# A bidirectional state-space scan: its within-chunk decay tables made during the attention and parked in DRAM

## The chip, the cores and the metric

The kernel runs on one core of one Trainium2 chip. The metric is the device time of one execution in microseconds (us), as the median of several runs; the profile is one more execution, recorded instruction by instruction. The engines are called PE (matrix products), DVE (vector work), ACT (activation functions and copies), POOL (the general engine, which also issues some DMAs) and SP (which issues most DMAs).

## The reference, cut to what matters

The program is two layers of a hybrid encoder: 1040 tokens (16 of them learned meta tokens), width 1024, all in float32. One input projection feeds four groups of 512 channels each: pooling, a 2-D Fourier transform, a bidirectional state-space scan (SSD) and attention. The group outputs are gated and go through one output projection, and the residual is added. The scan in one direction is

```
da  = dt * a                       # per token and head, 8 heads of 64 channels
cs  = cumsum(da)                   # within a chunk
L   = exp(cs[t] - cs[s])  for s <= t, else 0
y_diag = ((C B^T) * L) @ (x * dt)  # within the chunk
y_off  = C h_prev * exp(cs[t])     # from the chunks before
h      = h_prev * exp(cs[end]) + B^T (x * dt * exp(cs[end] - cs))
```

It runs forwards and backwards with separate dt and a, and the two are summed. For one chunk and one head the within-chunk part of both directions is one table of token s by token t, "decay times step size", multiplied by the product of B and C. That table depends on dt and a alone, not on x, B or C.

## The kernel before, in words

Chunks have 104 tokens (QC), ten of them (NQ). Every projection is done in float32 from high and low parts, three matmuls per product (mm3, lines 132 to 134), in column chunks of 348, 346 and 346 tokens. Generators yield after each step, and weave merges several of them in a fixed proportion; the program order that results is a priority, from which the framework orders each engine's queue. Buffers of one tag form a ring.

A layer goes through these stages. The attention handles four tiles t=0..3 of two heads: att_q and att_max of the next tile, att_main of this one (scores, exponentials L658, sums on POOL and DVE L668, products with v). The stream fill is woven in: input projections whose results are spilled to DRAM, in the order given by the string FO. U, P, F and Z are plain spills, C are the eight convolutions of the scan's input, R the Fourier projection, and D is spill_dt with ssd_dt. ssd_dt makes dt and its cumulative sums and stores them in DRAM: csd (cumulative sums by head), ecd (their exponentials), ded (chunk decays) and tkd (the same by token). After the attention come the Fourier transform and then the scan, both with output projections (outproj) woven in as the stream fill2; below, "fill" in the scan means these. outproj loads a 346-column piece into an sms buffer (L338), adds the product to it (DVE L352, or for the attention's part a copy on ACT L349 and an addition on POOL L350) and stores it (L353). The sms ring has four buffers.

ssd_load brings csd's companions and the convolved channels in. ssd_bwd goes through the chunks from the end and keeps the backward states. ssd_fwd has two halves per chunk. prepare(q) loads the cumulative sums, broadcast over 104 partitions, twice (L868, L869, 338 KB each, into two of five bb buffers rf and rb); transposes the chunk; makes C B^T for two groups (L876); masks it twice with DVE (L880 for s <= t, L881 for s >= t, into cfb); then for each of eight heads takes a minimum on DVE (L883) and an exponential on ACT (L884), scales one mask on ACT (L887) and adds the other, scaled, on DVE (L888); and multiplies both 104x832 tables on POOL (L889). finish(q) loads the exponentials of ecd into e (a buffer of the large ring, L897), multiplies the products with the states by it (L900, L903), updates the state (ssd_state: L808, L811, L817, L818), adds the within-chunk products (L914, L915) and the skip (L917). prepare(q+1) stands ahead of finish(q). ssd_fin normalises finished columns; the output projection of the scan's channels follows.

Of the kernel before, what the change touches and what calls it, by code (L numbers as in the profile page):

```python
# [27 lines left out]
QC = 104  # L28
# [24 lines left out]
def hybrid_trunk(ctx: ExitStack, tc: tile.TileContext, io, out, depth=DEPTH):  # L53
# [22 lines left out]
    PB, KB, NPF, NACC = 2, 3, 14, 4  # L76
# [5 lines left out]
    FK = 3  # L82
    FN = (9, 17, 17, 16, 27)
    PC = 8 // GK
    TP = 0
    FO = 'UPFDCCCCCRCCCZ'
# [6 lines left out]
    def nm(s):  # L93
        uid[0] += 1
        return f"{s}{uid[0]}"
# [12 lines left out]
    def chunk_tile(tag, dt=F32):  # L108
        return phase["p"].tile([128, 348], dt, name=nm(tag), tag=tag, bufs=NPF if tag == "pf" else PB)
# [694 lines left out]
    def ssd_state(s, i, q, x, bt, st, xw, new, tag="pv"):  # L804

        w = s.tok[q][:, 64 + 32 * i:72 + 32 * i].rearrange("p (a j) -> p j a", j=4)
        for a in range(2):
            nc.vector.tensor_tensor(hv(xw)[:, :, a], hv(x[:QC])[:, :, a], w[:, :, a].unsqueeze(2).broadcast_to([QC, 4, 64]), op=ALU.mult)  # L808
        p = ps(tag)
        for g in range(2):  # L810
            nc.tensor.matmul(p[:, g * 256:g * 256 + 256], bt[:, g * 128:g * 128 + 128], xw[:, g * 256:g * 256 + 256], start=True, stop=True)  # L811
        if st is None:
            nc.scalar.copy(new, p)
        else:
            d = s.decb[:, i, :, q].rearrange("p (a j) -> p j a", j=4)
            for a in range(2):
                nc.gpsimd.tensor_tensor(hv(new)[:, :, a], hv(st)[:, :, a], d[:, :, a].unsqueeze(2).broadcast_to([128, 4, 64]), op=ALU.mult)  # L817
            nc.vector.tensor_tensor(new, new, p, op=ALU.add)  # L818
        return new
# [8 lines left out]
    def ssd_load(l, s):  # L828
# [3 lines left out]
        s.gap = phase["p"].tile([QC, NQ, 8], F32, name=nm("gap"), tag="gap", bufs=1)  # L832
        for q0 in (0, 5):
            t = big()[:QC, :720].rearrange("t (q c) -> t q c", c=144)
            nc.sync.dma_start(t, s.tkd[q0:q0 + 5].rearrange("q t c -> t q c"))
            s.tok += [t[:, i] for i in range(5)]
            nc.vector.tensor_tensor(s.gap[:, q0:q0 + 5], t[:, :, 32:40], t[:, :, 0:8], op=ALU.subtract)
# [19 lines left out]
    def ssd_fwd(l, s):  # L857
        s.y = [s.xbc[j] for j in range(4)]
        mf, mb = ct[:QC, C_MF:C_MF + QC], ct[:QC, C_MB:C_MB + QC]
# [3 lines left out]
        def prepare(q):  # L863

            qs = slice(q * QC, (q + 1) * QC)
            tok = s.tok[q]
# [10 lines left out]
            cfb = phase["p"].tile([128, 4 * QC], F32, name=nm("cfb"), tag="cfb", bufs=1)[:QC].rearrange("p (g t) -> p g t", t=QC)  # L877
            cf, cb = cfb[:, 0:2], cfb[:, 2:4]
            pcv = pc[:QC, :2 * QC].rearrange("p (g t) -> p g t", t=QC)
            nc.vector.tensor_tensor(cf, pcv, mf.unsqueeze(1).broadcast_to([QC, 2, QC]), op=ALU.mult)  # L880
            nc.vector.tensor_tensor(cb, pcv, mb.unsqueeze(1).broadcast_to([QC, 2, QC]), op=ALU.mult)  # L881
            for r in range(8):
                nc.vector.scalar_tensor_tensor(rf[:, r], rb[:, r], s.gap[:, q, r:r + 1], rf[:, r], op0=ALU.add, op1=ALU.min)  # L883
                nc.scalar.activation(rf[:, r], rf[:, r], AF.Exp, bias=tok[:, r:r + 1])  # L884
            for r in range(8):
                g = (r % 4) // 2
                nc.scalar.activation(rb[:, r], cb[:, g], AF.Copy, scale=tok[:, 136 + r:137 + r])  # L887
                nc.vector.scalar_tensor_tensor(rb[:, r], cf[:, g], tok[:, 104 + r:105 + r], rb[:, r], op0=ALU.mult, op1=ALU.add)  # L888
            nc.gpsimd.tensor_tensor(rb, rb, rf, op=ALU.mult)  # L889
            ready[q] = (xt, xw, bt, rb)  # L890

        def finish(q, st):
            qs = slice(q * QC, (q + 1) * QC)
            xt, xw, bt, rb = ready.pop(q)
            e = vr(big())
            for a in range(2):
                nc.sync.dma_start(e[64 * a:64 * a + 64].rearrange("p (i j) t -> p i j t", i=2), s.ecd[q, :, 4 * a:4 * a + 4].partition_broadcast(64))  # L897
# [125 lines left out]
    for l in range(depth):  # L1023
# [11 lines left out]
        kv = att_kv(l, s)  # L1035
# [8 lines left out]
        for t in range(4):  # L1044
# [5 lines left out]
            if t < 3:  # L1050
                run(weave((att_main(l, s, t), LS + 3 * PC), (chain(*side), 20 + 3 * PC + 6), (islice(fill, n), n)))
# [147 lines left out]
```

## Time and profile before

| what | value |
| --- | --- |
| median of 3 runs | 2157.05 us (2153.55 to 2157.64) |
| profiled execution | 2152.37 us |
| its span | 2150.6 us |
| granted PE clock over the span | 0.97 |
| DMA | 261.01 MB, mean 121 GB/s |
| first and last start of the forward scan's L883 | 832.3 and 2078.3 us |

A row of the table by stretch holds the stretch, its length, and for each engine its busy time and number of instructions; then the clock granted to PE (1.00 is full speed), the mean busy share of the 16 DMA engines and GB/s. A row of a group reads: line, engine, operation, output and inputs by name, shape, count, then busy time in us, mean of one in ns, and the idle time of the engine before them with what ended it. A row of waits reads: who waited for whom, us in total, times, the longest in us. A row of one line reads: count, then minimum, median and maximum in ns.

### The profile page before, as it was taken

Reading aid. Unit: us, or ns where it says so; the run is one execution under the profiler, and the core shown is the slowest. Engines: PE = TensorE matmul, PEld = TensorE weight load, DVE = VectorE, ACT = ScalarE, POOL = GpSimd, SP = SyncE. Lnnn points to the kernel's source line nnn. Section 1 sums busy time; section 2 is a strip of 40 time slices with the busy share of each in tenths; the row PEclk is TensorE's granted clock in tenths of the full one; section 3 lists DMA queues with packets and bytes.
Section 4 is the critical chain, followed back from the end, with each engine's and each line's share of the span. In section 5 each row is a group of like instructions: output and inputs, shape, how many; then the busy total and the mean of one; then the engine's idle time right before and its main releaser. Section 6 shows DMA issues by size and latency. Waiting matters only on the chain. (4 is left out here: it accounts for less than half of the span.)

```text
span 2150.6 us, 33395 instructions
## 1 busy us (share of the span) xinstructions
PE 2008.4 (93%) x11880; PEld 1760.3 (82%) x11880; DVE 1397.7 (65%) x2785; ACT 1008.9 (47%) x2187; POOL 462.6 (22%) x465
## 2 busy tenths in 40 slices
PE   6999999999999888988889999999999998989888
PEld 5898988689889668877779988977888995778878
DVE  5675547767664455689795754476776634466996
ACT  5535344553543346346465343436534442463662
POOL 2013122031310200245230221221312111012550
PEclk9999999999999998998999999999999999989999
DMA  4322122122323377666643221212123335776666
GB/s 140 104 66 74 52 65 60 46 76 95 99 108 119 115 202 237 194 176 190 183 128 118 66 69 50 65 53 84 66 89 102 127 107 152 211 227 183 178 185 189
DMA packets 164605, 261.01 MB, mean 121 GB/s; under 512 B 20878, under 2 KB 113618, under 8 KB 164438
## 3 DMA queue, kind: packets, MB, share of 16 engines
q1 hardware_dynamic: 161782, 249.55, 38.2%
q0 software_dynamic: 2656, 9.33, 1.8%
q8 instruction: 93, 1.52, 0.3%
q14 instruction: 74, 0.61, 0.1%
HBM read 182.91 MB, written 71.67 MB: 118 GB/s over the span
## 5 line engine op out<-in xcount | busy, mean ns | idle before, releaser
L132 PE MATMUL psmm<-big,wh 128*128 128x346 f32 (+2 forms) x1920 | 644.9, 336 | 38.5 <-ACT big L128 14.8
L133 PE MATMUL psmm<-big,wh 128*128 128x346 f32 (+2 forms) x1920 | 634.6, 331 | 6.6 <-DVE big L129 3.3
L134 PE MATMUL psmm<-big,wl 128*128 128x346 f32 (+2 forms) x1920 | 628.5, 328 | 1.3 <-DVE wl L129 1.3
L132 PEld LDWEIGHTS psmm<-big,wh 128*128 128x128 f32 x1920 | 370.9, 193 | 85.1 <-issue 32.0
L133 PEld LDWEIGHTS psmm<-big,wh 128*128 128x128 f32 x1920 | 371.4, 193 | 18.8 <-DVE big L129 6.8
L134 PEld LDWEIGHTS psmm<-big,wl 128*128 128x128 f32 x1920 | 371.5, 194 | 4.8 <-DVE wl L129 2.4
L668 POOL TENSOR_TENSOR acc<-acc,pf 116x346 f32<-116x346 f32 (+5 forms) x216 | 222.4, 1042 | 695.4 <-ACT pf L658 553.4
L128 ACT CAST wh<-wr 128x512 fp32r<-128x512 f32 (+1 forms) x236 | 145.2, 616 | 272.4 <-PE psmm L133 197.9
L129 DVE TENSOR_TENSOR wl<-wr,wh 128x512 fp32r<-128x512 f32 x232 | 168.6, 731 | 132.6 <-ACT wh L128 131.7
L132 PE MATMUL psy<-big,wh 128*128 128x346 f32 (+2 forms) x672 | 221.0, 329 | 0.8 <-ACT big L187 0.5
L133 PE MATMUL psy<-big,wh 128*128 128x346 f32 (+2 forms) x672 | 218.2, 325 | 2.7 <-DVE big L188 2.0
L134 PE MATMUL psy<-big,wl 128*128 128x346 f32 (+2 forms) x672 | 217.0, 323 | 0.0
L658 ACT ACTIVATE pf<-psy 116x346 f32<-116x346 f32 (+4 forms) x288 | 125.4, 457 | 90.2 <-PE psy L656 88.1
L678 PE MATMUL pspv<-pf,vt 116*64 116x346 f32 (+5 forms) x864 | 166.0, 466 | 0.0
L668 DVE TENSOR_TENSOR acc<-acc,pf 116x346 f32<-116x346 f32 (+5 forms) x120 | 102.2, 852 | 83.0 <-ACT pf L658 62.2
L627 DVE TENSOR_REDUCE mx<-psy 116x1 f32<-116x346 f32 (+3 forms) x272 | 132.8, 511 | 16.0 <-PE psy L626 15.4
L132 PEld LDWEIGHTS psy<-big,wh 128*128 128x128 f32 x672 | 127.0, 189 | 10.9 <-issue 6.3
L133 PEld LDWEIGHTS psy<-big,wh 128*128 128x128 f32 x672 | 127.0, 189 | 8.2 <-DVE big L188 3.1
L134 PEld LDWEIGHTS psy<-big,wl 128*128 128x128 f32 x672 | 127.2, 189 | 0.6
L678 PEld LDWEIGHTS pspv<-pf,vt 116*64 116x64 f32 (+1 forms) x864 | 58.6, 136 | 61.2 <-issue 26.8
L627 DVE TENSOR_REDUCE mx<-pssc 128x1 f32<-128x346 f32 (+3 forms) x136 | 69.8, 513 | 41.5 <-PE pssc L626 39.8
L352 DVE TENSOR_TENSOR sms<-sms,psmm 128x346 f32<-128x346 f32 (+2 forms) x104 | 52.5, 509 | 67.9 <-PE psmm L134 46.8
(290 smaller groups left out, 3376.6 us busy)
## 6 DMA issues: line engine op xcount, KB each, us to landing
wr<-w SPq DMA_DIRECT2D x248, 256.0 KB
sms<-hd SPq DMA_DIRECT2D x112, 173.0 KB
hd<-sms SPq DMA_DIRECT2D x96, 173.0 KB
bb<-csd SPq DMA_DIRECT2D x40, 338.0 KB
md<-big SPq DMA_DIRECT2D x24, 520.0 KB
gd<-sms SPq DMA_DIRECT2D x64, 173.0 KB
big<-gd SPq DMA_DIRECT2D x16, 520.0 KB
big<-md SPq DMA_DIRECT2D x16, 520.0 KB
```

The source lines that it names most:

```text
L128: nc.scalar.copy(hi, src)
L129: nc.vector.tensor_tensor(lo, src, f(hi), op=ALU.subtract)
L132: nc.tensor.matmul(out_ps, ah, bh, start=start, stop=False)
L133: nc.tensor.matmul(out_ps, ah, bl, start=False, stop=False)
L134: nc.tensor.matmul(out_ps, al, bh, start=False, stop=stop)
L352: nc.vector.tensor_tensor(o, ht, p[:, :cw], op=ALU.add)
L627: nc.vector.tensor_reduce(mx[:qn, q, e, ci:ci + 1], p[:qn, :cw], axis=AX.X, op=ALU.max)
L658: nc.scalar.activation(pf[:n, :cw], p[:n, :cw], AF.Exp, scale=0.125)
L668: eng.tensor_tensor(accs[c0, e][:n, :cw], accs[c0, e][:n, :cw], pf[:n, :cw], op=ALU.add)
L678: nc.tensor.matmul(hold["pv"][64 * e:64 * e + 64, :cw], s.vt[:n, k, v, :], pfs[e][:n, :cw], start=(k == 0), stop=(k == len(KTS) - 1))
```

## The change

Four things change.

1. A new generator ssd_tab makes, per chunk and per half of the heads (four), the table exp(min(...)) * (mask * dt + other mask * dt) and stores it in DRAM (dec, 104x832 per chunk). It has 60 steps, three per half chunk, and is woven into the attention's tiles t=1 and t=2, 30 steps each (TT). Per half chunk: one load of csd into the single buffer tb, one addition and one product on POOL, one minimum and four scaled additions on DVE, four exponentials and four scaled copies on ACT, and one store that POOL issues. Per chunk there is one load of tkd into the single buffer tk and one subtraction on DVE.
2. prepare(q) loads the table in one DMA of 338 KB, and multiplies it by C B^T straight out of PSUM in two DVE products of 104x416. The masks, minima, exponentials, scalings and the POOL product go from the scan, as do cfb and gap.
3. The load of e moves from finish into prepare, and e takes a bb buffer in place of one of the large ring.
4. In ssd_state the two half operations on DVE (L808) and the two on POOL (L817) become one each over all heads. In FO the letter D moves ahead of P and F, so that ssd_dt is done by t=0; pf has 13 buffers instead of 14.

```diff
-    PB, KB, NPF, NACC = 2, 3, 14, 4
+    KB, NPF, NACC = 3, 13, 4
+    TT = (0, 30, 30)
-    FO = 'UPFDCCCCCRCCCZ'
+    FO = 'UDPFCCCCCRCCCZ'
...
+    def ssd_tab(l, s):
+        mf, mb = ct[:QC, C_MF:C_MF + QC], ct[:QC, C_MB:C_MB + QC]
+        s.dec = drp.tile([NQ, QC, 8 * QC], F32, name=nm("dec"))
+        for q in range(NQ):
+            tok = phase["p"].tile([QC, 152], F32, name=nm("tk"), tag="tk", bufs=1)
+            nc.sync.dma_start(tok[:, :144], s.tkd[q])
+            nc.vector.tensor_tensor(tok[:, 144:152], tok[:, 32:40], tok[:, 0:8], op=ALU.subtract)
+            for a in range(2):
+                t = phase["p"].tile([QC, 2, 4, QC], F32, name=nm("tb"), tag="tb", bufs=1)
+                rf, rb = t[:, 0], t[:, 1]
+                nc.sync.dma_start(t, s.csd[q, :, 4 * a:4 * a + 4].partition_broadcast(QC))
+                gap = tok[:, 144 + 4 * a:148 + 4 * a].unsqueeze(2).broadcast_to([QC, 4, QC])
+                nc.gpsimd.tensor_tensor(rb, rb, gap, op=ALU.add)
+                yield
+                nc.vector.tensor_tensor(rf, rf, rb, op=ALU.min)
+                for r in range(4):
+                    nc.scalar.activation(rf[:, r], rf[:, r], AF.Exp, bias=tok[:, 4 * a + r:4 * a + r + 1])
+                    nc.scalar.activation(rb[:, r], mb, AF.Copy, scale=tok[:, 136 + 4 * a + r:137 + 4 * a + r])
+                yield
+                for r in range(4):
+                    nc.vector.scalar_tensor_tensor(rb[:, r], mf, tok[:, 104 + 4 * a + r:105 + 4 * a + r], rb[:, r], op0=ALU.mult, op1=ALU.add)
+                nc.gpsimd.tensor_tensor(rf, rf, rb, op=ALU.mult)
+                nc.gpsimd.dma_start(s.dec[q, :, 4 * a * QC:4 * a * QC + 4 * QC], rf)
+                yield
...
     def ssd_state(s, i, q, x, bt, st, xw, new, tag="pv"):
-        for a in range(2):
-            nc.vector.tensor_tensor(hv(xw)[:, :, a], hv(x[:QC])[:, :, a], w[:, :, a].unsqueeze(2).broadcast_to([QC, 4, 64]), op=ALU.mult)
+        nc.vector.tensor_tensor(hv(xw), hv(x[:QC]), w.unsqueeze(3).broadcast_to([QC, 4, 2, 64]), op=ALU.mult)
...
-            for a in range(2):
-                nc.gpsimd.tensor_tensor(hv(new)[:, :, a], hv(st)[:, :, a], d[:, :, a].unsqueeze(2).broadcast_to([128, 4, 64]), op=ALU.mult)
+            nc.gpsimd.tensor_tensor(hv(new), hv(st), d.unsqueeze(3).broadcast_to([128, 4, 2, 64]), op=ALU.mult)
...
         def prepare(q):
-            rf, rb = vr(bb()[:QC]), vr(bb()[:QC])
-            nc.sync.dma_start(rf, s.csd[q, 0].partition_broadcast(QC))
-            nc.sync.dma_start(rb, s.csd[q, 1].partition_broadcast(QC))
+            rb, e = vr(bb()[:QC]), vr(bb())
+            nc.sync.dma_start(rb, s.dec[q].rearrange("s (r t) -> s r t", t=QC))
+            for a in range(2):
+                nc.sync.dma_start(e[64 * a:64 * a + 64].rearrange("p (i j) t -> p i j t", i=2), s.ecd[q, :, 4 * a:4 * a + 4].partition_broadcast(64))
...
-            for r in range(8):
-                nc.vector.scalar_tensor_tensor(rf[:, r], rb[:, r], s.gap[:, q, r:r + 1], rf[:, r], op0=ALU.add, op1=ALU.min)
-                nc.scalar.activation(rf[:, r], rf[:, r], AF.Exp, bias=tok[:, r:r + 1])
-            for r in range(8):
-                g = (r % 4) // 2
-                nc.scalar.activation(rb[:, r], cb[:, g], AF.Copy, scale=tok[:, 136 + r:137 + r])
-                nc.vector.scalar_tensor_tensor(rb[:, r], cf[:, g], tok[:, 104 + r:105 + r], rb[:, r], op0=ALU.mult, op1=ALU.add)
-            nc.gpsimd.tensor_tensor(rb, rb, rf, op=ALU.mult)
+            pcv = pc[:QC, :2 * QC].rearrange("p (g t) -> p g t", t=QC).unsqueeze(2).broadcast_to([QC, 2, 2, QC])
+            for a in range(2):
+                m = rb[:, 4 * a:4 * a + 4].rearrange("p (g i) t -> p g i t", g=2)
+                nc.vector.tensor_tensor(m, m, pcv, op=ALU.mult)
...
-                run(weave((att_main(l, s, t), LS + 3 * PC), (chain(*side), 20 + 3 * PC + 6), (islice(fill, n), n)))
+                run(weave((att_main(l, s, t), LS + 3 * PC), (chain(*side), 20 + 3 * PC + 6), (islice(fill, n), n), (islice(tab, TT[t]), TT[t] + 0.01)))
```

More of the change, by code (lines that the diff above doesn't have):

```diff
@@ L108, in chunk_tile @@
     def chunk_tile(tag, dt=F32):
-        return phase["p"].tile([128, 348], dt, name=nm(tag), tag=tag, bufs=NPF if tag == "pf" else PB)
+        return phase["p"].tile([128, 348], dt, name=nm(tag), tag=tag, bufs=NPF)
     def bb():
@@ L831, in ssd_load @@
         s.tok = []
-        s.gap = phase["p"].tile([QC, NQ, 8], F32, name=nm("gap"), tag="gap", bufs=1)
         for q0 in (0, 5):
@@ L836, in ssd_load @@
             s.tok += [t[:, i] for i in range(5)]
-            nc.vector.tensor_tensor(s.gap[:, q0:q0 + 5], t[:, :, 32:40], t[:, :, 0:8], op=ALU.subtract)
         s.xbc = [big() for _ in range(8)]
@@ L858, in ssd_fwd @@
         s.y = [s.xbc[j] for j in range(4)]
-        mf, mb = ct[:QC, C_MF:C_MF + QC], ct[:QC, C_MB:C_MB + QC]
         vr = lambda t: t[:, :8 * QC].rearrange("p (r t) -> p r t", t=QC)
@@ L865, in prepare @@
             qs = slice(q * QC, (q + 1) * QC)
-            tok = s.tok[q]
-            rf, rb = vr(bb()[:QC]), vr(bb()[:QC])
-            nc.sync.dma_start(rf, s.csd[q, 0].partition_broadcast(QC))
-            nc.sync.dma_start(rb, s.csd[q, 1].partition_broadcast(QC))
+            rb, e = vr(bb()[:QC]), vr(bb())
+            nc.sync.dma_start(rb, s.dec[q].rearrange("s (r t) -> s r t", t=QC))
+            for a in range(2):
+                nc.sync.dma_start(e[64 * a:64 * a + 64].rearrange("p (i j) t -> p i j t", i=2), s.ecd[q, :, 4 * a:4 * a + 4].partition_broadcast(64))
             px, bt = ssd_tok(s, q)
@@ L876, in prepare @@
                 nc.tensor.matmul(pc[:QC, g * QC:(g + 1) * QC], s.xbc[4 + g][:, qs], s.xbc[6 + g][:, qs], start=True, stop=True)
[L877 to L881, printed above, removed]
-            for r in range(8):
-                nc.vector.scalar_tensor_tensor(rf[:, r], rb[:, r], s.gap[:, q, r:r + 1], rf[:, r], op0=ALU.add, op1=ALU.min)
-                nc.scalar.activation(rf[:, r], rf[:, r], AF.Exp, bias=tok[:, r:r + 1])
-            for r in range(8):
-                g = (r % 4) // 2
[L887 to L890, printed above, removed]
+            pcv = pc[:QC, :2 * QC].rearrange("p (g t) -> p g t", t=QC).unsqueeze(2).broadcast_to([QC, 2, 2, QC])
+            for a in range(2):
+                m = rb[:, 4 * a:4 * a + 4].rearrange("p (g i) t -> p g i t", g=2)
+                nc.vector.tensor_tensor(m, m, pcv, op=ALU.mult)
+            ready[q] = (xt, xw, bt, rb, e)
         def finish(q, st):
             qs = slice(q * QC, (q + 1) * QC)
[L894 to L897, printed above, removed]
+            xt, xw, bt, rb, e = ready.pop(q)
             if q < NQ - 1:
@@ L1034, in hybrid_trunk @@
         s.md["x"] = drp.tile([8, 128, L], F32, name=nm("md"))
-        kv = att_kv(l, s)
+        kv, tab = att_kv(l, s), ssd_tab(l, s)
         if l == 0:
```

## The prediction, made before the changed kernel was run

> **What bounds the kernel now.** I read the page first, then the busy time by stretch, then, inside the scan, who waited for whom and the costliest groups.
>
> ```profile
> span 2150.6 us, 33395 instructions
> PE 2008.4 (93%) x11880; PEld 1760.3 (82%) x11880; DVE 1397.7 (65%) x2785; ACT 1008.9 (47%) x2187; POOL 462.6 (22%) x465
> ```
>
> PE is the bound of the whole, but 7% of 2150.6 us is not PE's. The stretches say where. The rows below are, in order: attention tiles t=1 and t=2 of layer 0, the same of layer 1 (cut at the stores of L718), the two forward scans, and the quieter stretch of layer 0 after t=2.
>
> ```profile
> core 0: us, PE busy (x) PEld busy (x) DVE busy (x) ACT busy (x) POOL busy (x), PEclk, DMA share, GB/s
> 288.00:440.00 152.00, 147.22 (x826) 119.59 (x825) 99.67 (x227) 73.60 (x169) 31.92 (x34) 0.99 0.20 60
> 440.00:570.00 130.00, 129.69 (x778) 111.01 (x777) 92.19 (x164) 61.06 (x130) 32.29 (x31) 1.00 0.24 79
> 1349.00:1496.00 147.00, 141.39 (x810) 115.07 (x809) 95.63 (x216) 71.71 (x163) 29.91 (x33) 1.00 0.20 60
> 1496.00:1627.00 131.00, 130.96 (x788) 112.70 (x787) 91.18 (x161) 62.24 (x131) 32.04 (x32) 1.00 0.24 80
> 885.00:1035.00 150.00, 133.42 (x884) 123.70 (x882) 124.98 (x296) 78.46 (x218) 65.05 (x60) 0.93 0.67 187
> 1970.00:2118.00 148.00, 132.01 (x889) 120.06 (x887) 130.35 (x301) 77.16 (x207) 65.83 (x58) 0.93 0.67 186
> 590.00:700.00 110.00, 107.53 (x657) 100.82 (x656) 58.41 (x91) 43.02 (x80) 12.01 (x10) 0.98 0.34 116
> ```
>
> In t=2 PE is busy 99.8% with DVE at 71%. In the scans PE falls to 89%, DVE stands at 83% and 88%, and the granted clock is 0.93. So the attention is PE's and the scan is where another engine sets the time. Who held PE up in the first scan:
>
> ```profile
> PE pspv L811 <- DVE big L903: 7.6, 6, 2.6
> PE psmm L132 <- ACT sms L349: 3.4, 2, 2.1
> PE pspv L811 <- DVE big L808: 2.2, 2, 1.9
> ```
>
> The 16.6 us that PE lacks there (150 minus 133.4) are mostly waits for DVE work that stood in DVE's queue. The change takes from exactly that queue and adds to the attention's.
>
> **The forward scan, terms.** These groups of the whole program (20 chunks in two layers) carry the price:
>
> ```profile
> L883 DVE SCALAR_TENSOR_TENSOR bb<-bb,gap,bb 104x104 f32<-104x104 f32 x160 | 65.0, 456 | 5.7 <-DMA bb<-csd 5.7
> L884 ACT ACTIVATE bb<-bb,big 104x104 f32<-104x104 f32 x160 | 50.6, 376 | 34.9 <-DVE bb L883 28.4 <-issue 6.2
> L888 DVE SCALAR_TENSOR_TENSOR bb<-cfb,big,bb 104x104 f32<-104x104 f32 x160 | 48.0, 356 | 1.3 <-ACT bb L887 1.2
> L887 ACT ACTIVATE bb<-cfb,big 104x104 f32<-104x104 f32 x160 | 46.0, 370 | 11.6 <-DVE cfb L881 11.3
> L889 POOL TENSOR_TENSOR bb<-bb,bb 104x832 f32<-104x832 f32 x20 | 41.7, 2084 | 61.0 <-DVE bb L888 61.0
> L880 DVE TENSOR_TENSOR cfb<-psy,ct 104x208 f32<-104x208 f32 x18 | 6.5, 364 | 1.2 <-PE psy L876 1.2
> L881 DVE TENSOR_TENSOR cfb<-psy,ct 104x208 f32<-104x208 f32 x18 | 6.5, 361 | 0.0
> L900 DVE TENSOR_TENSOR big<-pssc,big 128x416 f32<-128x416 f32 x18 | 10.5, 583 | 6.1 <-DMA big<-ecd 4.3 <-issue 1.1 <-PE psxx L914 0.7
> L903 DVE TENSOR_TENSOR big<-pspv,big 128x416 f32<-128x416 f32 x18 | 10.4, 580 | 3.7 <-DMA big<-ecd 3.7
> L808 DVE TENSOR_TENSOR big<-big,big 104x256 f32<-104x256 f32 x36 | 18.1, 532 | 3.3 <-ACT big L873 3.2
> L818 DVE TENSOR_TENSOR big<-big,pspv 128x512 f32<-128x512 f32 x24 | 16.3, 680 | 7.7 <-PE pspv L811 7.7
> ```
>
> Busy time over count (neighbours overlap, so it is below the mean). DVE, removed per chunk: eight L883 (65.0/20 = 3.25 us), eight L888 (48.0/20 = 2.40), one L880 and one L881 (0.72): 6.37. Added: two products of 104x416 from PSUM with SBUF. No such instruction is shown; the nearest is L900, 128x416 from PSUM at 0.583, so 1.17. One 512-wide L808 for two of 256 (0.532 each, or 1.06): nearest is L818 with 512 columns, 0.68, so 0.38 less. Net 5.58 us a chunk, 56 a layer. About nine chunks lie in the first stretch and eight in the second: 125 minus 50 leaves 75 us of DVE, 130 minus 45 leaves 85. ACT loses 16 operations a chunk, (50.6+46.0)/20 = 4.8 us; POOL loses L889, 2.08 us. L817's two halves become one: the same elements, nothing counted.
>
> The exponent load e (L897) moves from the head of finish into prepare, one chunk earlier. Its late landings held DVE 4.3 + 3.7 us, in the rows of L900 and L903; these go. Against that, rb and e now both live in the ring of five bb buffers until finish ends, where rf was free after L889, so SP's load for chunk q waits for chunk q-2's products. One 338 KB load instead of two relieves a DMA share of 0.67. I set the ring's wait at nothing because a whole chunk (15 us) lies between; should that cover go, a 4 to 5 us landing shows per chunk.
>
> PE's own work does not change. Its matmuls run slower in the scan:
>
> ```profile
> L132 PE MATMUL psmm<-big,wh 128*128 128x346 f32 (+1 forms) x161 | 55.8, 346 | 4.4 <-ACT sms L349 3.4 <-DVE sms L352 1.0
> L132 PE MATMUL psmm<-big,wh 128*128 128x346 f32 (+1 forms) x113 | 37.2, 329 | 0.0
> ```
>
> (first in the scan, second in t=2): 346 against 329 ns, 5% longer at the granted 0.93. With fewer gaps I give back 3%: 133.4 becomes 129.4, and 132.0 becomes 128.1. What share PE then reaches: DVE would stand at 55 to 63%, and the row with that load, 590:700 (53%), has PE at 97.8%. That is the upper bound. The lower is 0.91, little above today's 0.89, if the state chain and the fill (the output projection's tiles woven into the scan) hold. I take 0.95, nearer the quiet row, since the scan keeps its chain L811, L818, L825, L903. 129.4/0.95 = 136.2 and 128.1/0.95 = 134.8: gains of 13.8 and 13.2, together **27 us** (bounds 15 and 35).
>
> **The attention, terms.** The tables' 60 steps go into t=1 and t=2, ten half-chunks each.
>
> ```profile
> L668 POOL TENSOR_TENSOR acc<-acc,pf x216: 891/934/4068, 149.5 to 1805.7; 116x346 f32<-116x346 f32 x64, 116x348 f32<-116x348 f32 x16, 116x332 f32<-116x332 f32 x16, 112x346 f32<-112x346 f32 x8
> L668 DVE TENSOR_TENSOR acc<-acc,pf x120: 490/990/1254, 149.9 to 1812.2; 116x346 f32<-116x346 f32 x64, 116x348 f32<-116x348 f32 x16, 112x346 f32<-112x346 f32 x16, 116x332 f32<-116x332 f32 x16
> L627 DVE TENSOR_REDUCE mx<-psy x272: 498/509/522, 113.0 to 1610.9; 116x1 f32<-116x348 f32 x48, 128x1 f32<-128x348 f32 x40, 116x1 f32<-116x346 f32 x24, 128x1 f32<-128x346 f32 x24
> L621 POOL DMA_DIRECT2D big<-big x16: 509/547/708, 117.9 to 1562.5; - x16
> DMA to landing us min/median/max: 2.9/3.2/4.6
> 365.00:400.00 35.00, 33.21 (x160) 21.32 (x159) 30.50 (x85) 10.44 (x31) 4.75 (x5) 1.00 0.08 21
> ```
>
> DVE per half-chunk: one minimum of 104x416, by L668 (346 columns) 0.49 to 0.99, scaled 0.59 to 1.19; four scaled adds at 0.30 to 0.41 (L888, L883 per instruction): 1.8 to 2.8. Middle 2.3, or 23 us a tile. ACT: eight operations at about 0.3, 24 us a tile, to some 65% of the stretch; not a bound. POOL: two of 104x416 at half of L889, 1.04 each, and one store issue at 0.55: 26 us a tile, from 32 to 58. DVE in t=2: 92 + 23 = 115 of 130, 89%.
>
> The dt work (order letter D) moves from t=1 into t=0. The last row is its stretch: DVE 87%, PE 94.9%. That is also the only attention stretch with the DVE load that t=2 will have, so I take 0.95 for PE in t=2: 129.7/0.95 = 136.5 and 131.0/0.95 = 137.9, **13.4 us** lost in both layers (bounds: nothing if PE keeps its 99.8%, 32 if it falls to the scan's 0.89). In t=1, 99.7 + 23 minus some 10 of D's excess is 74%: no more than now, nothing counted. In t=0 D costs what it cost in t=1: a move, net nothing.
>
> Waits that are added: the single tb buffer. SP's load of the next half waits until POOL's store has landed. The chain is store 0.55 + 3.2, load about 4.3 (below), POOL 1.04, DVE 1.2, ACT 2.4, DVE 1.2 to 1.6, POOL 1.04: about 15 us, against a pace of (152+130)/20 = 14.1. It just misses; but nothing reads the tables before the scan, so they may run on into t=3. What stands behind: on SP the weight loads, on POOL the sums L668 that free pf (13 buffers now).
>
> ```profile
> 1947.16 4.33 DMA bb<-csd
> SPq L205 <- DVE wl L129: 60.0, 13, 13.1
> L658 ACT ACTIVATE pf<-psy 116x346 f32<-116x346 f32 (+4 forms) x288 | 125.4, 457 | 90.2 <-PE psy L656 88.1 <-POOL acc L668 0.8
> ```
>
> SP already stands up to 13 us in t=2 for a free weight buffer, so loads run well ahead: cover. pf's ring held ACT 0.8 us in the whole program: cover.
>
> **A rule against the change.** DVE's 0.49 to 0.99 us for one L668 depends on what POOL does meanwhile. The Trainium skill (SBUF — State Buffer, "SBUF: two separate sides") says that GpSimd and a DVE operation with two SBUF inputs exclude each other for a whole instruction. By that rule the middle of 2.3 is too low, and the sum is the first rival's. The trace agrees in kind: L668 with two operands in SBUF doubles, L627 with one in PSUM does not stretch; no row shows the lock itself.
>
> **Sum.** The profiled execution took 2152.37 us, 1.8 outside its span. 2152.4 - 27 + 13.4 = 2138.8. The median of the runs, 2157.05, lies 4.7 above it, and I carry that: **2143 us**.
>
> **Rivals.** (1) DVE becomes the bound of t=2. Twenty new POOL operations a tile at 1.04 each hold DVE up: 115 + 21 = 136 us of DVE, at most 88% dense (the highest row, the second scan): 154.5 for 130, so 24.5 a layer, 49 in all, minus 27: 2179. For it: L668's median at twice its minimum. Against: the row of L627 above, the largest DVE user of the attention, never longer than 522 ns. It decides once t=2 loses 13.5 us a layer, that is DVE work above 126, half of the 21. Chance 0.17. (2) The scan is not DVE's but the fill's: each output tile needs two of four sms buffers, and SP waited
>
> ```profile
> SPq L353 <- POOL sms L350: 48.0, 21, 6.6
> SPq L338 <- DMA hd<-sms: 19.4, 16, 3.0
> ```
>
> in the first scan. Then PE goes to 0.91 only, 15 us, and the attention's 13 eat it: 2155, no measurable change. Against: L350 stands behind L889 in POOL's queue, which goes. Chance 0.15. (3) The scan reaches 97.8% and the attention hides everything: 35 less, 2122. Chance 0.2. Forecast: 0.48.
>
> **From cases to numbers.** What a measurement can tell from no change is about 0.2%, 4.3 us. Faster: nearly all of the forecast and of (3), 0.65. Same: most of (2) and the forecast's edge, 0.13. Slower: (1) and what is worse of (2), 0.22. The range runs from case (3) to two thirds of the way to case (1): 2122 to 2168.
>
> **What would show it.** Right: L883 to L889 gone from the scan, DVE there about 75 us, PE share 0.95, the scan about 136 us; t=2 about 136 us with DVE near 0.9; the clock near 0.97. Wrong: a scan still at 145 us or more, with SP or L349 ahead of PE; or a t=2 above 144 us with L627 or L668 late.

## The result and the profile after

The changed kernel takes 2215.64 us (median of 4 runs, 2208.17 to 2228.89), the kernel before took 2157.35 beside it: a ratio of 1.0282 as estimated over the runs (the two medians alone give 1.027), 95% interval 1.0243 to 1.0321. By the medians it is 58 us slower, where 14 us faster was forecast, and lies outside the range (2122 to 2168). The profiled execution of after took 2228.89 us, 13 above the median of its runs, so times are compared by the medians of the runs, and the profile is read for stretches, waits and gaps.

The page of after, its first lines and the shares of the chain that ended last:

```profile
span 2227.1 us, 33333 instructions
PE 2032.1 (91%) x11880; PEld 1765.4 (79%) x11880; DVE 1378.8 (62%) x2645; ACT 989.6 (44%) x2179; POOL 518.4 (23%) x533
PE psmm L133 7%; PE psmm L134 6%; PE psmm L135 6%; DMA tb<-csd 6%; DMA sms<-hd 4%; PE pspv L679 4%; DMA hd<-sms 3%; PE psy L133 3%; PE psy L135 3%; PE psy L134 3%; DMA dec<-tb 3%; DMA big<-fw 1%; PE psy L627 1%; DMA sms<-md 1%; POOL tb L800 1%
```

The load of the table's source (tb<-csd) and the store of the table (dec<-tb) now hold 9% of the chain. No other engine became busier than PE: DVE stands at 62%.

The busy time by stretch, first of before and then of after, over the same piece of work: from the first chunk's product of C and B in the forward scan to the ninth's, layers 0 and 1. The columns are as in the prediction.

```profile
882.50:1018.10 135.60, 121.26 (x793) 112.79 (x794) 110.58 (x265) 64.08 (x181) 56.46 (x53) 0.92 0.67 186
1937.20:2069.40 132.20, 119.09 (x795) 110.90 (x794) 108.50 (x261) 63.01 (x179) 56.80 (x53) 0.93 0.67 184
```

```profile
941.50:1062.60 121.10, 112.79 (x795) 105.54 (x794) 69.39 (x129) 30.32 (x60) 35.51 (x35) 1.00 0.65 179
2028.90:2145.00 116.10, 111.08 (x794) 104.37 (x794) 68.72 (x130) 29.94 (x60) 35.50 (x35) 1.00 0.67 186
```

The same 794 matmuls take 14.5 and 16.1 us less. DVE fell from 82% of the stretch to 57%, and the granted clock rose from 0.92 to 1.00. The scan does what was forecast.

The attention does not. The stretches of after are t=0, t=1 and t=2 of layer 0, then of layer 1, cut at the stores that close a tile:

```profile
146.00:314.00 168.00, 154.14 (x848) 126.76 (x848) 110.98 (x255) 89.22 (x230) 50.43 (x54) 0.95 0.27 80
314.00:486.50 172.50, 151.13 (x841) 125.69 (x840) 103.60 (x201) 83.70 (x219) 64.23 (x68) 0.96 0.28 87
486.50:630.00 143.50, 136.96 (x794) 117.68 (x793) 98.46 (x180) 65.23 (x146) 39.89 (x40) 0.96 0.25 81
...
1245.00:1413.40 168.40, 156.74 (x881) 128.36 (x880) 118.56 (x269) 88.99 (x227) 52.28 (x56) 0.97 0.28 82
1413.40:1578.00 164.60, 145.81 (x834) 123.17 (x832) 96.25 (x191) 79.27 (x211) 56.10 (x64) 0.97 0.29 88
1578.00:1718.00 140.00, 134.37 (x778) 115.23 (x779) 96.66 (x175) 66.67 (x149) 37.97 (x40) 0.97 0.25 81
```

t=1 of layer 0 grew from 152 to 172.5 us, t=2 from 130 to 143.5, and t=0, which was to hold no table step, ends at 313.7 us where it ended at 287.7 before. All three tiles of the two layers lost about 108 us in this execution, counted from the first score product of t=0 (at 142.0 and 1209.5 us before, at 142.9 and 1251.6 now). DVE is busy 58 to 70% of these stretches, so it is no saturated engine that holds PE. PE has gaps, and its clock is below 1.

**Who stands and waits.** The answer on the tile tb in after, whole run: the engine's idle time just before an instruction on tb, by who waited and for whom (us, times):

```profile
L789 SPq DMA_DIRECT2D tb<-csd x40: 300/322/820, 202.1 to 1607.7; - x40
...
  DMA tb<-csd: 166.3, 35
  DVE tb L793: 156.5, 35
  POOL tb L791: 121.5, 34
  DVE tb L799: 115.7, 30
```

POOL stood 166 us for the loads, ACT 156 us for DVE's minimum, DVE 121 us for POOL's addition, POOL 116 us again for DVE's sums. The first load was issued at 202.1 us, in t=0, though the program asks for it only in t=1. One half chunk shows what that means. DVE from 340 to 352 us (start, duration, instruction; in brackets the idle time before it and what ended it):

```profile
339.38 1.06 DVE L669 TENSOR_TENSOR acc<-acc,pf 112x348 f32<-112x348 f32 x1
344.67 0.59 DVE L793 TENSOR_TENSOR tb<-tb 104x416 f32<-104x416 f32 x1 [4.23 <-POOL tb L791]
345.99 0.33 DVE L799 SCALAR_TENSOR_TENSOR tb<-ct,tk,tb 104x104 f32<-104x104 f32 x1 [0.72 <-ACT tb L796]
...
350.20 1.15 DVE L667 TENSOR_TENSOR acc<-pf,pf 116x346 f32<-116x346 f32 x1 [2.25 <-ACT pf L659]
```

SP, POOL and ACT in the same time:

```profile
340.18 0.32 SPq L789 DMA_DIRECT2D tb<-csd  x1
```

```profile
343.76 0.88 POOL L791 TENSOR_TENSOR tb<-tb,tk 104x416 f32<-104x416 f32 x1 [3.70 <-DMA tb<-csd]
348.09 1.07 POOL L800 TENSOR_TENSOR tb<-tb 104x416 f32<-104x416 f32 x1 [3.45 <-DVE tb L799]
```

```profile
345.30 0.38 ACT L795 ACTIVATE tb<-tb,tk 104x104 f32<-104x104 f32 x1 [7.97 <-DVE tb L793]
...
347.82 0.79 ACT L659 ACTIVATE pf<-psy 116x346 f32<-116x346 f32 x2
```

The load is issued at 340.18 and lets POOL begin at 343.76. For nearly all that time three engines have an instruction on tb at the head of their queues, and what stands behind it waits too. ACT does nothing for 7.97 us, and behind the eight table operations and one copy stands L659, the exponentials that empty the score banks in PSUM. When it runs, at 347.82, PE has run dry. PE's first instruction after the gap, and PE by stretch:

```profile
348.32 0.64 PE L656 MATMUL psy<-big,big 128*116 128x346 f32 x1 [2.72 <-ACT pf L659]
```

```profile
346.00:348.30 2.30, 0.00 (x0) 0.00 (x0) 1.29 (x4) 2.30 (x9) 0.21 (x1) 1.00 0.00 0
348.30:350.00 1.70, 1.68 (x6) 1.68 (x7) 0.00 (x0) 1.67 (x5) 1.40 (x2) 0.51 0.31 104
350.00:352.00 2.00, 2.00 (x8) 1.61 (x7) 1.77 (x2) 0.78 (x2) 0.95 (x2) 0.57 0.27 87
352.00:356.00 4.00, 4.00 (x28) 3.02 (x27) 0.07 (x1) 2.23 (x5) 0.46 (x1) 1.00 0.53 152
```

PE does nothing for 2.72 us, to 348.32, and then it works for some 3.4 us at half its clock (0.51, 0.57): six and eight matmuls in 3.7 us, where the next 4 us hold 28. So a gap is paid for twice. The waits of PE in after between 150 and 640 us begin

```profile
PE psy L656 <- ACT pf L659: 17.1, 8, 4.2
PE psxx L771 <- DVE big L767: 4.4, 2, 4.1
```

where before's list for the same time begins

```profile
PE psxx L132 <- ACT smn L128: 2.5, 2, 2.1
```

and has 0.8 us for the exponentials L658 in all. Two numbers sum this up, and the experiments use them: the time in which PE was idle, and the time lost to the clock, both added up over stretches of 2 us (2 minus PE's busy time, and 2 times one minus the granted clock). Over both attentions (146 to 700 us and 1240 to 1800) before has 24 and 7 us, after 83 and 39. The growth, 91 us, is most of the 108.

### The profile page after: what moved, and what is told of

It is laid out like the page before. It is cut to its first block, busy times and chain, and to the rows that moved or that the text cites. A ratio compares the mean times of both kernels' runs of the same rounds, so it can differ in the third digit from the quotient of the medians.

```text
span 2227.1 us, 33333 instructions
## 1 busy us (share of the span) xinstructions
PE 2032.1 (91%) x11880; PEld 1765.4 (79%) x11880; DVE 1378.8 (62%) x2645; ACT 989.6 (44%) x2179; POOL 518.4 (23%) x533
## 4 chain that ended last, share of the span: by engine, by line
PE 45%; DMA 22%; DVE 14%; ACT 8%; POOL 5%; issue 4%; SPq 1%; POOLq 0%; DVEq 0%; ACTq 0%
PE psmm L133 7%; PE psmm L134 6%; PE psmm L135 6%; DMA tb<-csd 6%; DMA sms<-hd 4%; PE pspv L679 4%; DMA hd<-sms 3%; PE psy L133 3%; PE psy L135 3%; PE psy L134 3%; DMA dec<-tb 3%; DMA big<-fw 1%; PE psy L627 1%; DMA sms<-md 1%; POOL tb L800 1%
## 5 line engine op out<-in xcount | busy, mean ns | idle before, releaser
L133 PE MATMUL psy<-big,wh 128*128 128x346 f32 (+2 forms) x688 | 229.4, 334 | 0.8 <-ACT big L188 0.5
L134 PE MATMUL psy<-big,wh 128*128 128x346 f32 (+2 forms) x688 | 226.7, 329 | 2.6 <-DVE big L189 2.2
L135 PE MATMUL psy<-big,wl 128*128 128x346 f32 (+2 forms) x688 | 224.9, 327 | 0.1
L659 ACT ACTIVATE pf<-psy 116x346 f32<-116x346 f32 (+4 forms) x288 | 125.4, 457 | 51.7 <-PE psy L657 48.5
L133 PEld LDWEIGHTS psy<-big,wh 128*128 128x128 f32 x688 | 133.3, 194 | 11.6 <-issue 7.8
L134 PEld LDWEIGHTS psy<-big,wh 128*128 128x128 f32 x688 | 133.0, 193 | 8.2 <-DVE big L189 3.5
L135 PEld LDWEIGHTS psy<-big,wl 128*128 128x128 f32 x688 | 133.0, 193 | 1.6 <-issue 0.5
L656 PE MATMUL psy<-big,big 128*116 128x346 f32 (+4 forms) x288 | 100.4, 349 | 35.3 <-ACT pf L659 29.3
L795 ACT ACTIVATE tb<-tb,tk 104x104 f32<-104x104 f32 x160 | 59.7, 373 | 159.7 <-DVE tb L793 156.5
```

The lines of the kernel that those rows point to most:

```text
L133: nc.tensor.matmul(out_ps, ah, bh, start=start, stop=False)
L134: nc.tensor.matmul(out_ps, ah, bl, start=False, stop=False)
L135: nc.tensor.matmul(out_ps, al, bh, start=False, stop=stop)
L656: nc.tensor.matmul(p[:n, :cw], k1[:, k0:k0 + n], s1[e][:, cs], start=True, stop=False)
L659: nc.scalar.activation(pf[:n, :cw], p[:n, :cw], AF.Exp, scale=0.125)
```

## The experiments

The theory drawn from these two traces was that the attention's side, not the scan's, holds the loss, and that engines standing for the table's chain are its cause (theory A made the single tb buffer the reason). The rivals: the work itself, the moved letter D with the shorter pf ring, and the queue orders that the framework makes. All ratios are against the kernel before on the same chip.

**Each side alone.** The scan's side: the tables aren't made, and the scan loads as many bytes from elsewhere.

```diff
-    TT = (0, 30, 30)
+    TT = (0, 0, 0)
...
-            nc.sync.dma_start(rb, s.dec[q].rearrange("s (r t) -> s r t", t=QC))
+            nc.sync.dma_start(rb, io["w1"][l, q, 0:QC].rearrange("p k c -> p (k c)")[:, :8 * QC].rearrange("s (r t) -> s r t", t=QC))
```

> Only the scan's side of the change: the tables are not made (that part is left out), and each chunk's table load takes as many bytes of the input weights instead, so what the scan multiplies by is not the decay. All else as in the changed kernel. Theory A (the loss sits in the attention, where one buffer makes each half chunk's load wait for the store before it, and POOL, DVE and ACT stand in order behind that load): the scan's gain shows by itself, about 34 us as the two traces differ outside the attention, so 2157 - 34 = 2123, ratio 0.984. Rival B (the added work itself, DVE and POOL getting in each other's way): the same here, 0.984. Rival C (the earlier dt work and the smaller pf ring cost the time): the loss stays, ratio above 1.02.

Measured: 2116.08 us, 0.9809 (0.9795 to 0.9824): 41 us gained. The attention's side: before's scan, with ssd_tab, FO and pf as in after, and the tables never read. Against before:

```diff
+    TT = (0, 30, 30)
+    def ssd_tab(l, s):
...
```

> Only the attention's side: the scan of the kernel before, with the tables made in the attention and stored but not read. Order of the dt work and pf ring as in the changed kernel. A and B: the whole loss without the scan's gain, about 2157 + 92 to 110, ratio 1.043 to 1.051. C: the same loss. A counterpart (the loss arises in the scan, for example from the shared bb ring): ratio below 1.01.

Measured: 2256.78 us, 1.0465 (1.0433 to 1.0498): 100 us lost. 100 minus 41 is 59, and the change lost 58: the sides add up. In the profile the loss lies in the attention alone: from the first score product to the last it is 59 and 54 us longer than before in the two layers, and what follows takes the same time within 1 us.

**Order and ring alone.** Before, with only D moved and pf at 13.

```diff
-    PB, KB, NPF, NACC = 2, 3, 14, 4
+    PB, KB, NPF, NACC = 2, 3, 13, 4
...
-    FO = 'UPFDCCCCCRCCCZ'
+    FO = 'UDPFCCCCCRCCCZ'
```

> The kernel before with only the dt work moved ahead in the fill's order and pf at 13 buffers; no tables in the attention, the scan as before. A and B: within 0.3% of the kernel before (2151 to 2163). C: much of the loss, ratio above 1.02.

Measured: 2157.38 us, 1.0004 (0.9988 to 1.0021). The prediction's "a move, net nothing" and "cover" hold: in layer 0, t=0 takes 155.4 us instead of 145.7, and t=1 143.2 instead of 151.9.

**Two tb buffers.** One buffer of the large ring pays for it.

```diff
-                t = phase["p"].tile([QC, 2, 4, QC], F32, name=nm("tb"), tag="tb", bufs=1)
+                t = phase["p"].tile([QC, 2, 4, QC], F32, name=nm("tb"), tag="tb", bufs=2)
...
-    NBIG, NBB = 30, 5
+    NBIG, NBB = 29, 5
```

> The changed kernel with two tb buffers instead of one; to make room the ring of large buffers goes from 30 to 29. A: the load of the next half chunk no longer waits for the store, POOL's wait for the load (166 us in the changed kernel) falls below 60, DVE's for POOL (121) below 50, and at least two thirds of the 92 to 110 us come back: 2120 to 2165, ratio below 1.004. B: the work is the same, so the time stays near 2216 (ratio 1.02 to 1.03). C: the same as B.

Measured: 2225.51 us, 1.0318 (1.0296 to 1.0340): no gain, and theory A fell. On tb:

```profile
L789 SPq DMA_DIRECT2D tb<-csd x40: 300/322/681, 195.8 to 1497.5; - x40
...
  DVE tb L799: 100.5, 35
  DVE tb L793: 70.7, 20
  DMA tb<-csd: 56.5, 20
  POOL tb L791: 46.0, 23
```

The waits fell as A said, POOL's for the load from 166 to 56 us and DVE's for POOL from 121 to 46; these four together fell from 560 to 274 us. The time did not follow: PE was idle for 173 us of the whole run and lost 97 to the clock, 270 in all, against after's 194 and 72 and before's 142 and 65. The last load went out at 1497.5 us instead of 1607.7, so the tables were made in less time, all within t=0 and t=1. So the sum of the waits on tb does not measure the loss; what stands behind each of them counts. What the large ring's missing buffer costs was not measured alone.

**Work without the chain, chain without the work.** First all the operations of ssd_tab on constants and tiles of their own, no DMA, no hop; then the same DMAs and hops with operations one column wide, one on ACT and one on DVE in place of each eight and four. The scan is before's in both, and the first is kept in program order (its meaning comes with the next experiment). The minimum stands for all, first in the one, then in the other.

```diff
-                nc.vector.tensor_tensor(rf, rf, rb, op=ALU.min)
+                tc.keep_in_program_order(nc.vector.tensor_tensor(od, c4(0), c4(104), op=ALU.min))
```

```diff
-                nc.vector.tensor_tensor(rf, rf, rb, op=ALU.min)
+                nc.vector.tensor_tensor(rf[:, :, 0:1], rf[:, :, 0:1], rb[:, :, 0:1], op=ALU.min)
```

> The attention's side alone (scan of the kernel before), with all the table's work on POOL, DVE and ACT in the same shapes, but each engine reads constants and writes a small tile of its own: no load, no store, no engine waits for another (the tables are left out). Each operation is kept at its place in the program's order, or it would move to the start. The full attention side alone took 2257, 100 more than before. Two buffers gave nothing back, so the single buffer is out. Theory A2 (engines stand at the head of their queues for the chain load, POOL, DVE, ACT, DVE, POOL, store, one or two buffers alike): a loss below 30, under 2187. Theory B (the work itself: time on ACT, DVE and POOL lengthens the attention's loop through its few PSUM banks): a loss above 70, over 2227.

> The counterpart: the same loads, stores, single buffer and chain of engines in the attention, scan of the kernel before, but each operation covers one column per head and the eight on ACT and four on DVE become one each (the tables are left out). A2: a loss above 60, over 2217. B: below 30, under 2187.

Measured: 2182.45 us, 1.0110 (1.0077 to 1.0142), and 2201.17 us, 1.0205 (1.0168 to 1.0242). The work costs 23 us, as theory A2 in the expectations (engines stand for the chain) said. The chain with next to no work costs 42, less than A2's 60 and more than its rival's 30, so it decides for neither. The remaining 35 of the 100 come only when both are there. Perhaps a hop that waits for real work takes longer and more stands behind it; this is not shown, and the two runs differ in their order too, since only the work was bound to the program's.

**Order kept, pace slower.** Each instruction of ssd_tab is bound to its place in the program; in the second kernel, with the new TT, the tables are also spread over t=3.

```diff
-                nc.gpsimd.tensor_tensor(rb, rb, gap, op=ALU.add)
+                tc.keep_in_program_order(nc.gpsimd.tensor_tensor(rb, rb, gap, op=ALU.add))
...
-    TT = (0, 30, 30)
+    TT = (0, 18, 18, 24)
```

> The changed kernel with every instruction of the tables kept behind what the program has put on its engine before it, so the framework cannot move it forward into t=0 and into gaps that it takes to be free. Same work, same chain. If the loss comes from where the queues' order puts the table's operations: under 2190. B: no change, 2205 to 2230. A2 with nothing but the chain: 2200 or more, since the chain still takes some 14 us per half chunk at a pace of 14.1.

> As the run before, with the 60 steps spread as 18, 18 and 24 over t=1, t=2 and t=3 instead of 30 and 30. A2: the chain then has 24 us per half chunk, the waits at the queues' heads go, and the time falls by 15 or more against that run. B: the same work, within 6 us of that run.

Measured: 2203.02 us, 1.0204 (1.0173 to 1.0235), and 2181.79 us, 1.0106 (1.0074 to 1.0139). Keeping the order alone brings some 15 us (13 by the medians, 17 by the ratios, which come from two chips), the slower pace another 21.

**One hop per step.** A yield after the load, after POOL's addition, after the minimum with ACT's eight, after DVE's sums: 120 steps a layer instead of 60, so that other work lies between a producer and its consumer on each queue. First kept in order; then later in the attention, with TT = (0, 24, 32, 64); then the first one with the order left to the framework, whose edit is shown.

```diff
                 nc.sync.dma_start(t, s.csd[q, :, 4 * a:4 * a + 4].partition_broadcast(QC))
+                yield
...
                 nc.vector.tensor_tensor(rf, rf, rb, op=ALU.min)
+                yield
...
-    TT = (0, 30, 30)
+    TT = (0, 36, 36, 48)
```

> The changed kernel with each hop of the chain in a step of its own (load, POOL sum, DVE minimum, ACT, DVE, POOL product with store: 120 steps, spread as 36, 36 and 48 over t=1 to t=3, so some 4 us between hops), each instruction kept at its place in the program's order; the one subtraction per chunk comes after the load's step. Same work, one buffer. A2 (waits of one engine at the head of its queue for the hop before): DVE's wait for POOL and ACT's for DVE fall below 20 us each over the program, and only the work's share of the loss stays (23 as measured without the chain) less the scan's 41: 2130 to 2155, ratio below 0.999. B: as the slower pace alone, 2175 to 2190.

> As the run before, with the steps spread as 24, 32 and 64: more of the tables' work in t=3, where DVE has the most room. A2: the same as that run within 8 us, since the hops are 4 us or more apart in t=1 and t=2 and about 2 to 3 us in t=3. B: faster than that run by 10 or more, as t=1 and t=2 have less work.

> As the first run of this call, but the framework may move the tables' instructions forward again. A2 with the order as its cause: the chain runs back to back from t=0 on, as in the changed kernel, and the loss returns: above 2185. If only the spacing in the program matters: as the first run, below 2160.

Measured: 2166.59 us, 1.0055 (1.0038 to 1.0071); 2156.94 us, 1.0001 (0.9983 to 1.0019); and 2214.93 us, 1.0260 (1.0222 to 1.0298). The first and the last are the same program but for the binding, and lie 48 us apart. Against the slower pace alone (1.0106) the spaced hops bring another 11 us by the ratios. The first is between what the two theories forecast for it, and so is the second, 9.7 us faster than the first. On tb, in the kernel kept in order and then in the free one:

```profile
L788 SPq DMA_DIRECT2D tb<-csd x40: 322/328/1457, 255.4 to 1856.9; - x40
...
  DVE tb L802: 144.8, 38
  DMA tb<-csd: 109.7, 20
  POOL tb L793: 33.5, 18
...
  DVE tb L795: 26.4, 13
```

```profile
L788 SPq DMA_DIRECT2D tb<-csd x40: 301/322/790, 199.2 to 1605.1; - x40
...
  DMA tb<-csd: 165.1, 36
  DVE tb L795: 157.5, 35
  POOL tb L793: 122.1, 35
```

Left free, the framework issues the first load at 199.2 us instead of 255.4 and the last at 1605.1 instead of 1856.9, and the waits are those of after. In the kept kernel POOL still stands 145 us for DVE's sums and 110 for the loads. What fell is ACT's wait for DVE's minimum, from 157 to 26 us, and DVE's for POOL's addition, from 122 to 34 (below 20 was expected for each): the two queues that hold the exponentials and the reductions. PE's longest entry in layer 0's attention in after, L656 for L659 with 17.1 us in eight waits, is 5.6 us in three. So the spacing must be there, and the queues must keep it: either alone brings some 15 us or nothing. Over the whole run PE's idle time and lost clock are 179 and 82 us in the free kernel, 148 and 63 in the kept one, 144 and 60 in the later one, which is level with before.

**Finer steps.** ACT's eight and DVE's four cut in half, 160 steps, kept in order.

```diff
                 for r in range(4):
...
+                    if r % 2:
+                        yield
...
+    TT = (0, 32, 40, 88)
```

> As the hop-per-step kernel kept in order, with the eight ACT operations and the four DVE additions of a half chunk split into two steps each (160 steps, spread as 32, 40 and 88 over t=1 to t=3). A2 with bursts as what is left: PE waits less behind four or eight operations in a row, 2140 to 2152, ratio below 0.999, faster than both kernels. B alone (the work's time, however it is cut): 2153 to 2165.

Measured: 2175.13 us, 1.0089 (1.0060 to 1.0119), slower than with whole hops and than either theory forecast. PE's idle time and lost clock rose to 165 and 77 us; which wait brings them wasn't told apart.

**The work, engine by engine.** ssd_tab's operations of one engine alone, on constants, kept in order, with before's scan. POOL's addition stands for the others:

```diff
-                nc.gpsimd.tensor_tensor(rb, rb, gap, op=ALU.add)
+                tc.keep_in_program_order(nc.gpsimd.tensor_tensor(op, c4(0), c4(104), op=ALU.add))
```

> The kernel before with the earlier dt work and, in the attention, only the tables' ACT operations (eight of 104x104 per half chunk, on constants, into a tile of their own, kept in order); the tables are left out. If ACT in the way of the exponentials is the work's cost: 12 us or more (over 2168). If not: under 6.

> The same with only DVE's operations (one minimum of 104x416 and four additions of 104x104 per half chunk, one of 104x8 per chunk); the tables are left out. If DVE in the way of the maxima is the cost: 12 us or more. If not: under 6.

> The same with only POOL's two operations of 104x416 per half chunk; the tables are left out. If POOL's exclusion of DVE is the cost (the prediction's first rival): 12 us or more, with DVE's sums of two SBUF operands (mean 852 ns before) longer by 50 ns or more. If not: under 4, and the mean as before.

Measured: ACT 2158.5 us, 1.0007 (0.9993 to 1.0022); DVE 2160.6 us, 1.0020 (1.0004 to 1.0037); POOL 2173.76 us, 1.0070 (1.0045 to 1.0094). POOL's 40 operations a layer are the dearest, 15 us, and the three together cost about 21 of the work's 23. DVE's groups with POOL's work alone, and then in the kernel with order and ring alone, which has none:

```profile
L628 DVE TENSOR_REDUCE mx<-psy 116x1 f32<-116x346 f32 (+3 forms) x272 | 133.0, 511 | 32.0 <-PE psy L627 31.3
L669 DVE TENSOR_TENSOR acc<-acc,pf 116x346 f32<-116x346 f32 (+5 forms) x120 | 113.9, 949 | 70.5 <-ACT pf L659 56.0 <-POOL acc L669 13.1
```

```profile
L627 DVE TENSOR_REDUCE mx<-psy 116x1 f32<-116x346 f32 (+3 forms) x272 | 133.3, 511 | 33.9 <-PE psy L626 33.3
L668 DVE TENSOR_TENSOR acc<-acc,pf 116x346 f32<-116x346 f32 (+5 forms) x120 | 102.0, 850 | 77.0 <-ACT pf L658 62.5 <-POOL acc L668 13.2
```

The same DVE sums with both operands in SBUF take 949 ns instead of 850, the reductions out of PSUM 511 in both. That fits in kind the rule of the Trainium skill that the prediction weighed ("SBUF — State Buffer", section "SBUF: two separate sides"): a POOL and a DVE operation with two inputs in SBUF hold each other up. It is no proof: POOL's own sums hardly change (1056 ns against 1040), and in the run with the work of all three engines, POOL's included, the same DVE sums take 820 ns. How the 15 us arise is not shown.

**Without POOL.** The hop over POOL is taken out: its addition goes into DVE's minimum (four operations), and its product to DVE; POOL only issues the store. Then the same with the product left on POOL.

```diff
-                nc.gpsimd.tensor_tensor(rb, rb, gap, op=ALU.add)
-                nc.vector.tensor_tensor(rf, rf, rb, op=ALU.min)
+                for r in range(4):
+                    tc.keep_in_program_order(nc.vector.scalar_tensor_tensor(rf[:, r], rb[:, r], tok[:, 144 + 4 * a + r:145 + 4 * a + r], rf[:, r], op0=ALU.add, op1=ALU.min))
...
+    TT = (0, 20, 28, 52)
```

> As the kernel with spaced hops, kept in order and spread late (2157), but POOL computes nothing: its sum goes into DVE's minimum (four operations of 104x104, each adding the gap and taking the minimum, as the scan did before), its product becomes one DVE operation, and POOL only issues the store. 100 steps, spread as 20, 28 and 52. If POOL's exclusion of DVE counts within the chain as it does alone: 12 us or more off 2157 less some 4 for the added DVE work, 2140 to 2150, faster than both kernels. If the chain's waits are what is left: 2153 to 2162.

> As the run before, but the product stays on POOL; only the sum moves into DVE's operations. If POOL's time is what counts, half of the gain of the run before, 2147 to 2154. If the length of the chain counts, the same as that run, since both have one engine change less at the start.

Measured: 2159.65 us, 1.0015 (1.0000 to 1.0030), and 2165.89 us, 1.0053 (1.0035 to 1.0071). Neither gains on the later spacing with POOL (1.0001), and the second is 6 us slower than the first, which neither of its forecasts had. So POOL's 15 us are not simply there to be saved once the chain is spaced; why not is open. No kernel that makes the tables in the attention beats the kernel before; the best of them is level with it.

Side by side, the profiled execution of each kernel split up for PE over the whole run; the rest is what PE's work takes at full clock, and the same work in all:

| kernel | span, us | PE idle | lost to the clock | rest |
| --- | --- | --- | --- | --- |
| before | 2151 | 142 | 65 | 1944 |
| after | 2227 | 194 | 72 | 1961 |
| scan alone | 2114 | 123 | 43 | 1948 |
| attention alone | 2263 | 207 | 108 | 1949 |
| work, no chain | 2179 | 167 | 67 | 1945 |
| chain, no work | 2199 | 170 | 86 | 1943 |
| kept in order | 2205 | 175 | 79 | 1952 |
| hop per step, kept | 2164 | 148 | 63 | 1952 |
| the same, later | 2152 | 144 | 60 | 1947 |
| the same, order free | 2218 | 179 | 82 | 1957 |
| POOL alone | 2169 | 160 | 71 | 1938 |

The rest stays within 24 us while the span moves by 150: but for that much, every large gain and loss of this study is a change in how long PE stands, and in how long it runs at half clock. Differences of 20 us and less are not told apart by this split.

## Why the prediction was wrong

**The scan.** Right, and too low: 41 us on its own against 27, above its bound of 35. The forward scan's two stretches gave 14.5 and 16.1 where 13.8 and 13.2 were forecast (for stretches some 15 us longer); the mis-sized term in them is the clock. "I give back 3%" for PE's matmuls; over the same 794 matmuls PE's busy time fell from 121.26 to 112.79 us, 7%. In before's first stretch the clock cost 10 us, in after's nothing: before it fell to 0.50 there four times, at gaps of 1.9 to 2.7 us, and the changed kernel has no gap above 1.73 us there. Over the whole run the scan's side alone takes 19 us from PE's idle time and 22 from the clock's loss; the prediction had priced about 8 of the latter. DVE's new work cost about what was said, 0.579 us a product against 0.583 and 0.765 for L834 against 0.68; the groups of after by shape:

```profile
L902 DVE TENSOR_TENSOR bb<-bb,psy 104x416 f32<-104x416 f32 x36 | 19.9, 579 | 0.0
...
L834 DVE TENSOR_TENSOR big<-big,big 104x512 f32<-104x512 f32 x18 | 13.6, 765 | 1.2 <-ACT big L895 1.2
```

In the profile of the scan's side alone, what follows the attention is 21 us shorter in each layer; 14 and 18 us of it lie between the first product of C and B and the last within-chunk product, the other 9 in small parts before and behind. Rival (2), the fill's ring, didn't come: the scan reached a PE share of 0.93 and 0.96.

**The attention.** This step failed: 100 us against 13.4, bounds 0 and 32. It priced the tables by how full DVE would be ("DVE in t=2: 115 of 130, 89%", so PE's share is that of a stretch with such a load), took the whole 13.4 from t=2, and counted nothing in t=0 and t=1. Against the kernel with order and ring alone, the profile of after has, over the two layers, 28 us more in t=0, 55 more in t=1 and 20 more in t=2 (170.8 and 161.6 us against 155.4 and 148.6; 172.5 and 164.6 against 143.2 and 138.5; 143.4 and 140.0 against 132.8 and 131.1). So four fifths of the loss lie in tiles that were counted at nothing. DVE in t=2 stood at 69%, not 89%: of a layer's 20 half chunks 7 were loaded in t=0, 11 in t=1 and 2 in t=2. The load that the price rested on never came, and PE lost more than the price. The prediction's own sign of failure, a t=2 above 144 us, did not come either, for it looked in the wrong tile.

What the runs show in its place: the work alone costs 23 us, the chain of hops with next to no work 42, and 35 more come only with both. A share of busy time could not show what the chain costs, because an engine that stands with a table instruction at its head is counted as idle.

**"About 15 us, against a pace of 14.1 ... they may run on into t=3".** The length was about right. The tile tb in layer 0:

```profile
L789 SPq DMA_DIRECT2D tb<-csd x20: 301/322/820, 202.1 to 513.3; - x20
```

Nineteen steps in 311.2 us are 16.4 us each; the tables were done in t=2, not in t=3, because they had begun in t=0. The error was to ask only whether the tables would be ready in time. Nobody waits for the tables, but for each hop of the chain an engine waits, and behind it the exponentials and reductions that PE needs. "What stands behind: on SP the weight loads, on POOL the sums" named the queues of the two ends and left out ACT and DVE in the middle: PE's longest entry among its waits is for ACT's L659.

**"In t=0 ... net nothing", "in t=1 nothing counted".** The move of D is nothing (1.0004). But the framework moved the tables' instructions too: the program order is a priority, the first load left at 202.1 us, and t=0 got 7 of 20 half chunks of layer 0. Holding them back is worth some 15 us with the hops as they are, and 48 once the hops are spaced.

**Rivals.** (1) forecast the right sign with another mechanism. POOL's operations alone cost 15 us, with DVE's sums 99 ns longer, but DVE was never the bound, and in after the same sums took 836 ns, no more than the 850 without any table:

```profile
L669 DVE TENSOR_TENSOR acc<-acc,pf 116x346 f32<-116x346 f32 (+5 forms) x120 | 100.3, 836 | 62.6 <-ACT pf L659 55.2 <-POOL acc L669 6.3
```

(3) was half right: the scan gave more than 35, and the attention hid nothing.

**Open.** Why half steps cost more than whole hops; why POOL's removal gains nothing in the spaced chain; where the 35 us come from that neither work nor chain has alone; and, in the best spaced kernel, which waits take back the scan's gain. Its profile shows where they lie: the attention is 14 us longer than before in each layer, the stretch from there to the scan's first state product 7 us longer, and all that follows 21 and 20 us shorter. Against the scan alone it has 21 us more of PE idle and 18 more lost to the clock.

## What to carry to other kernels

Idle share on an engine was no cover here for a chain that hops between engines: each hop blocked what stood behind it on its queue for as long as its producer took, a load's latency included. So ask for every hop which engine will stand at its head and what the bound engine needs from behind it. Here moved work came out level only with other instructions between its hops and with queues that kept that spacing: read the first start of the moved instructions in the trace to see where the framework really put them. Time a change's gaining side and its paying side apart; here 41 gained and 100 paid were one number.

## What the runs showed of the hardware

A gap on PE costs more than its length. In after's attention of layer 0, all eight gaps of PE from 2.63 to 4.23 us, and one of five from 1.38 to 2.13 us, were followed by 3.41 or 6.83 us at a granted clock of 0.50, or 1.7 or 3.4 us lost each; some of these stretches began before the gap had ended. In before's and after's traces the granted clock is 0.50 or 1.00 and nothing between, and it falls only at multiples of 3.41 us, counted from its first fall. The Trainium skill ("TensorE: Matmul & The Clock Gate", section "Part 1: The HAM clock gate (the "warmup" mystery)") says that the clock halves after an idle window of about 3.4 us. The half agrees, and so does 3.4 us as the step in time. But no gap of that length is needed: the gap of 2.72 us in the rows above was enough, and in before's first scan one of 1.93 us was. Over the whole run the clock cost 65 us before and 108 with the attention's side alone.

A load of 338 KB that repeats rows of DRAM over 104 partitions let its consumer begin 3.6 us after its issue (340.18 to 343.76), in the one case shown, with the DMA engines busy for 0.34 of that time.
